# State-space stage: conditioning tiles at fixed places of TensorE's order, input groups by halves, an eighth of the tables on GpSimd

## The chip, the cores and the metric

The kernel runs on one core of a Trainium2 chip. TensorE multiplies matrices and transposes, VectorE (DVE) and ScalarE (ACT) work elementwise, GpSimd (POOL) does so too, SyncE (SP) issues most loads. The metric is the device time of one execution in microseconds. Before the change three runs took 1083.6, 1089.24 and 1095.2 us.

## What is computed

Two transformer blocks over 256 positions of 1024 channels. The first begins with a norm modulated by conditioning vectors (`ada`), a state-space mixer (S5) and its gated output, then a feed-forward stage (FFN), latent attention and a second FFN; the second block has a recurrent time mix and differential attention. The change lies in the mixer:

```python
u = modulate(rms_norm(x, norm1_g), shift, scale)      # conditioning
s[t] = a * s[t-1] + bb @ u[t]                         # 64 complex states per group of 16 channels
y = Re(c @ s) + d_skip * u
g = gelu(y); mix = g * sigmoid(g @ w_glu + b_glu)     # GLU
```

Of `ada` come shift and scale of the norm (8 tiles, `adaH`), the gates and the modulation of the FFN (16 tiles, `ada0`), and further on those of the other stages (`kvada`, `ada1`, ...).

## The kernel before, in words

**The stage.** `s5()` unrolls the recurrence into chunks of 8 positions. A loop over e = 0 to 7 (four of 32 input groups each) makes on VectorE the table P (FP, the factors, times s5bc, the input matrices: four products and two sums a step, lines L803ff), turns it on TensorE into Bm, multiplies it with the output matrices (`cbd`) into KTr, and takes conditioning tiles by `pump` (L829). GpSimd makes the output tables CE (L831ff). The modulated input `xs` is transposed to U (L843ff). `into(j2)` multiplies U with Bm, `turnG(j2)` transposes the result and ScalarE copies it to GT; `pipe` runs the two over j2 = 0 to 3, turnG a step behind. ScalarE then loads its table for the Gelu (L886). The scan (L888 to L920) is a chain of products and sums on VectorE over the states St. `kernels(i)`, i = 0 to 3, builds the matrices Kmat within a chunk from KTr: transposes, a split into `kparts` (cast on ScalarE, rest on VectorE), 14 shifting matmuls, copies by ScalarE. Then TensorE adds up U times Kmat and St times CE (`outputs`), ScalarE applies the Gelu (gT), which is split in two (`gh` on ScalarE, `gl` = gT - gh on VectorE, L422), and `proj` runs the GLU: 192 matmuls on `gh`, `gl` and the likewise split weights `whi` (ScalarE), `wlo` (VectorE).

**The conditioning tiles.** 24 tiles of 1 MB, `adaH` and `ada0`, are each used in four matmuls into `ps_gv` (`gemv_rows`, `gemv`). Each `pump()` takes the next; a ring of three buffers `raw` holds them, so tile n + 3 is loaded when tile n has been used. Behind them come tiles that are accumulated on VectorE instead (`acc`, L323), the first of them `kvada`; `self.after` names an instruction behind which those have to stay.

**What sets the order.** A scheduler orders each engine's instructions by its own estimates; TensorE's alone stands as written within `manual_schedule` (the tables' loop up to the end of `pipe`, and the outputs with the Gelu's transposes). `tc.issue_after(x)` lets what is inside be issued behind x. Engines take their instructions in order: one that waits holds up those behind it. SP's loads of the stage are one queue. A buffer's next load waits until its last user is done; the GLU's weights lie where the states (`A`) and the tables (`CE`) lay.

In the rows L327 is a matmul, L330 a transpose, L306, L323 and L319 are VectorE's elementwise operations, L298 and L376 ScalarE's activations and casts, L357 the load of a weight tile.

Of the kernel before, what the change touches and what calls it, by code (L numbers as in the profile page):

```python
# [9 lines left out]
F32 = mybir.dt.float32  # L10
# [6 lines left out]
D, T, FF = 1024, 256, 2816  # L17
# [43 lines left out]
O_ORDER = [0, 1, 2, 3, 6, 7, 4, 5]  # L61

# [73 lines left out]
def pack(inp):  # L136
# [4 lines left out]
    a["xs"] = x.reshape(32, 8, 4, 16, 16)[:, ::-1].transpose(2, 0, 3, 1, 4).reshape(128, WT)  # L141
# [3 lines left out]
    w = ada[0][:, :2048].reshape(8, 128, 2, 4, 256).transpose(0, 1, 3, 2, 4)  # L145
# [6 lines left out]
    hb = adb[0][:2048].reshape(2, 4, 256).transpose(1, 0, 2).reshape(4, 512)  # L152
    a["modH"] = np.concatenate([rep(hb), rep(i["norm1_g"][0].reshape(4, 256))], 1)
# [135 lines left out]
class K:  # L289
# [130 lines left out]
    def split(self, hi, lo, src, eng=None):  # L420

        self.nc.scalar.copy(out=hi, in_=src)  # L422
        self.sub(lo, src, hi.bitcast(F32), eng)
# [221 lines left out]
    def s5(self):  # L645
# [3 lines left out]
        with ExitStack() as ctx:  # L649
# [130 lines left out]
            def kernels(i):  # L780
# [8 lines left out]
                self.pump()  # L789
                for t2 in (5, 3, 1, 0):  # L790
                    if t2 in (1, 3):
                        self.pump()
# [10 lines left out]
            self.pump()  # L803
            for e in range(8):
                Pq = B8("P", [128, 2, 4, 8, 16], "P", 4)
                g4 = slice(4 * e, 4 * e + 4)
                fv = lambda r: FP[:, r, :, g4].rearrange("p t g -> p g t").unsqueeze(3).to_broadcast([128, 4, 8, 16])
                bv = lambda r: bc[:, r, g4, :].unsqueeze(2).to_broadcast([128, 4, 8, 16])
                for r, (b0, b1, op) in enumerate(((0, 1, ALU.subtract), (1, 0, ALU.add))):
                    m1 = self.ps().rearrange("p (g t e) -> p g t e", g=4, t=8)  # L810
# [18 lines left out]
                self.pump(2 if e % 3 == 1 else 1)  # L829

            CE = [[B8("CE", [128, 16, 8, 16], f"CE{r}{i}", 4) for i in range(2)] for r in range(2)]
            for e in range(8):
# [3 lines left out]
                for r, (p0, p1) in enumerate(((0, 1), (2, 0))):  # L836
# [4 lines left out]
                    self.sub(ce, ce, m1, G)  # L841

# [4 lines left out]
            for h in range(2):  # L847
# [4 lines left out]
                for j4 in range(2):  # L852
# [4 lines left out]
                    o = U[:, 8 * h + 4 * j4:8 * h + 4 * j4 + 4].rearrange("p j n -> p (j n)")  # L857
                    (S_.copy if j4 else V.tensor_copy)(out=o, in_=pt)
# [16 lines left out]
            def turnG(j2):  # L875
                pt = self.ps("aux")
                for jl in range(2):
                    for ri in range(2):
                        self.T(pt[:, 128 * (2 * ri + jl):128 * (2 * ri + jl) + 128], gs_[j2][:, jl, ri, :])
# [4 lines left out]
            self.pipe(4, [into, turnG])  # L884
            order.close()
            self.table(AF.Gelu_apprx_tanh)  # L886
# [8 lines left out]
            S_.copy(out=St[:, 1::8], in_=GT[:, 0::8])  # L895
# [26 lines left out]
            for i in range(4):  # L922
                kernels(i)
# [1331 lines left out]
```

## Time and profile before

| | before |
|---|---|
| three runs, median | 1089.24 us (1083.6 to 1095.2) |
| the profiled execution | 1079.3 us |
| its span, first to last instruction | 1077.5 us |
| mean granted TensorE clock | 0.98 |
| TensorE busy | 985.0 us (91%) |
| VectorE busy | 809.5 us (75%) |
| ScalarE, GpSimd busy | 580.3 and 268.9 us |

The profile describes one execution. Times in the rows are microseconds from the span's start. A timeline row gives start, length, engine, line, operation, output and inputs with the size of one operation; equal operations that follow one another are merged (x8); in brackets stands how long the engine was idle before it and what released it. The clock is a share of 2.4 GHz, its full level; 0.50 is 1.2 GHz.

### The profile page before, as it was taken

Reading aid. Unit: us, or ns where it says so; the run is one execution under the profiler, and the core shown is the slowest. Engines: PE = TensorE matmul, PEld = TensorE weight load, DVE = VectorE, ACT = ScalarE, POOL = GpSimd, SP = SyncE. Lnnn points to the kernel's source line nnn. Section 1 sums busy time; section 2 is a strip of 40 time slices with the busy share of each in tenths; the row PEclk is TensorE's granted clock in tenths of the full one; section 3 lists DMA queues with packets and bytes.
Section 4 is the critical chain, followed back from the end, with each engine's and each line's share of the span. In section 5 each row is a group of like instructions: output and inputs, shape, how many; then the busy total and the mean of one; then the engine's idle time right before and its main releaser. Section 6 shows DMA issues by size and latency. Waiting matters only on the chain.

```text
span 1077.5 us, 21985 instructions
## 1 busy us (share of the span) xinstructions
PE 985.0 (91%) x8490; PEld 876.3 (81%) x8490; DVE 809.5 (75%) x1771; ACT 580.3 (54%) x1301; POOL 268.9 (25%) x300
## 2 busy tenths in 40 slices
PE   3988979999999988989999999988898899799996
PEld 1446968989999866889999999987887786699984
DVE  8846788989985788779756555688887735686995
ACT  6344555556544767646555544565444344575663
POOL 7960200030011551100000001453315132243430
PEclk9999989999999989999999999999999999999999
DMA  7999439877983241255755554241312142265321
GB/s 280 375 343 372 172 142 396 307 285 294 363 329 153 98 162 73 79 196 203 267 192 174 184 195 152 104 148 54 123 40 83 36 154 99 87 232 180 134 79 40
DMA packets 29416, 198.82 MB, mean 185 GB/s; under 512 B 3744, under 2 KB 3872, under 8 KB 6528
## 3 DMA queue, kind: packets, MB, share of 16 engines
q1 hardware_dynamic: 27936, 191.73, 48.2%
q10 hardware_dynamic: 720, 3.15, 0.8%
q0 software_dynamic: 656, 2.53, 0.7%
q8 instruction: 67, 1.10, 0.4%
q14 instruction: 37, 0.30, 0.1%
HBM read 195.30 MB, written 2.10 MB: 183 GB/s over the span
## 4 chain that ended last, share of the span: by engine, by line
PE 65%; DVE 15%; issue 4%; ACT 3%; POOL 2%; DMA 1%; POOLq 0%; DVEq 0%; ACTq 0%
PE ps_mm L327 50%; PE ps_aux L327 6%; DVE wlo L306 3%; PE ps_sv L327 3%; PE ps_el L327 2%; PE ps_aux L330 2%; PE ps_st L327 2%; ACT whi L376 1%; POOL sq L306 1%; DVE Upr L306 1%; DVE acc L323 1%; DMA raw<-in_gu 1%; DVE D L1738 1%; DVE shf L319 1%; DVE A L306 0%
## 5 line engine op out<-in xcount | busy, mean ns | idle before, releaser
L376 ACT CAST whi<-raw 128x512 fp32r<-128x512 f32 (+2 forms) x488 | 296.1, 613 | 271.5 <-PE ps_mm L327 230.0
L306 DVE TENSOR_TENSOR wlo<-raw,whi 128x512 fp32r<-128x512 f32 (+2 forms) x412 | 289.1, 714 | 128.4 <-ACT whi L376 127.7
L327 PE MATMUL ps_mm<-hh,whi 128*128 128x256 f32 x1064 | 306.8, 290 | 3.0 <-ACT hh L298 2.3
L327 PE MATMUL ps_mm<-hh,wlo 128*128 128x256 f32 x1064 | 300.6, 285 | 3.4 <-DVE wlo L306 3.3
L327 PE MATMUL ps_mm<-hl,whi 128*128 128x256 f32 x1064 | 300.0, 283 | 0.2
L327 PEld LDWEIGHTS ps_mm<-hh,whi 128*128 128x128 f32 x1064 | 202.0, 190 | 8.2 <-ACT hh L298 2.9
L327 PEld LDWEIGHTS ps_mm<-hh,wlo 128*128 128x128 f32 x1064 | 200.9, 190 | 8.8 <-DVE wlo L306 7.8
L327 PEld LDWEIGHTS ps_mm<-hl,whi 128*128 128x128 f32 x1064 | 201.9, 190 | 1.3 <-DVE hl L323 0.6
L306 POOL TENSOR_TENSOR wlo<-raw,whi 128x512 fp32r<-128x512 f32 (+2 forms) x76 | 100.3, 1321 | 244.1 <-ACT whi L376 218.5
L306 POOL TENSOR_TENSOR sq<-sq 128x256 f32<-128x256 f32 x20 | 23.4, 1171 | 415.0 <-ACT sq L298 264.7
L327 PE MATMUL ps_mm<-ah,whi 128*128 128x256 f32 x352 | 99.1, 282 | 0.0
L327 PE MATMUL ps_mm<-ah,wlo 128*128 128x256 f32 x352 | 99.0, 282 | 0.1
L327 PE MATMUL ps_mm<-al,whi 128*128 128x256 f32 x352 | 98.8, 281 | 0.0
L323 DVE SCALAR_TENSOR_TENSOR acc<-raw,cs,acc 128x512 f32<-128x512 f32 x112 | 80.0, 757 | 2.2 <-DMA raw<-in_kvada 2.1
L327 PEld LDWEIGHTS ps_mm<-ah,wlo 128*128 128x128 f32 x352 | 66.3, 189 | 2.8 <-issue 1.7
L327 PEld LDWEIGHTS ps_mm<-ah,whi 128*128 128x128 f32 x352 | 67.3, 191 | 0.9 <-ACT whi L376 0.8
L327 PEld LDWEIGHTS ps_mm<-al,whi 128*128 128x128 f32 x352 | 66.4, 189 | 0.0
L327 PE MATMUL ps_gv<-raw,crep 128*32 128x512 f32 x192 | 27.3, 624 | 17.0 <-DMA raw<-in_adaH 13.7
L327 PEld LDWEIGHTS ps_gv<-raw,crep 128*32 128x32 f32 x192 | 4.5, 110 | 22.0 <-DVE pwt L306 13.7
L327 PE MATMUL ps_mm<-gl,whi 128*128 128x256 f32 x64 | 18.9, 297 | 2.4 <-DVE gl L306 2.4
L327 PE MATMUL ps_mm<-whi,ch 128*128 128x512 f32 x48 | 19.5, 437 | 1.2 <-ACT ch L422 1.2
L306 POOL TENSOR_TENSOR CE<-CE,cem 128x512 f32<-128x512 f32 x16 | 20.5, 1321 | 0.0
(552 smaller groups left out, 2037.3 us busy)
## 6 DMA issues: line engine op xcount, KB each, us to landing
raw<-in_gu SPq DMA_DIRECT2D x44, 1024.0 KB, 5.1
raw<-in_ada SPq DMA_DIRECT2D x32, 1024.0 KB, 7.2
raw<-in_dn SPq DMA_DIRECT2D x22, 1024.0 KB, 5.0
raw<-in_win SPq DMA_DIRECT2D x15, 1024.0 KB, 4.9
raw<-in_adaH SPq DMA_DIRECT2D x8, 1024.0 KB, 6.4
raw<-in_kvada SPq DMA_DIRECT2D x8, 1024.0 KB, 6.5
raw<-in_ada1h SPq DMA_DIRECT2D x8, 1024.0 KB, 5.7
raw<-in_wout SPq DMA_DIRECT2D x8, 1024.0 KB, 4.9
```

The source lines that it names most:

```text
L306: return (eng or self.nc.vector).tensor_tensor(out=out, in0=a, in1=b, op=op)
L319: (eng or self.nc.vector).tensor_scalar(out=out, in0=a, scalar1=s1, scalar2=s2, op0=op0, **kw)
L323: return self.nc.vector.scalar_tensor_tensor(out=out, in0=a, scalar=s, in1=b, op0=op0, op1=op1, **kw)
L327: return self.nc.tensor.matmul(out, l, r, start=start, stop=stop, **kw)
L330: return self.nc.tensor.transpose(out, in_, self.ident)
L376: i = self.nc.scalar.copy(out=hi[:, :width], in_=raw[:, o:o + width])
L1738: V.tensor_reduce(out=D_[64 * h:64 * h + 64, 4 * i:4 * i + 4], in_=dm[:, :, h].rearrange("p c b i -> p c i b"), axis=AX.X, op=ALU.add)
```

## The change

- **Conditioning tiles.** The tables' loop takes one tile per step (8, and one ahead of it) instead of one or two; `pipe` becomes a loop over its five steps with a tile behind each, in TensorE's fixed order; kernels(1) to (3) take three, three and two. The last two of the 24 are taken within the GLU.
- **kernels(0)** is split: its transposes (`latest(0)`) stand behind step 5 of the tables' loop, its 14 matmuls behind step 7, both in the fixed order. kernels(1) to (3) follow the scan in the program and lie behind the last transposes of turnG.
- **Tables.** Step 3 of the eight (`GP`) is made on GpSimd, from `FPs`, a copy of FP that ScalarE makes. GpSimd's CE follows it.
- **Halves.** `S5_ORDER` permutes input columns, on the host, so that the first half of `xs` holds what into(0) and into(1) need. U is copied by ScalarE alone.
- **Order.** The load of the Gelu's table follows the copy into St; the scan's instructions follow turnG's last transposes. `self.after` is set before the GLU to the last split: no accumulation on VectorE goes before it.

```diff
--- before.py
+++ after.py
@@ -59,6 +59,10 @@
 O_ORDER = [0, 1, 2, 3, 6, 7, 4, 5]
+
+S5_ORDER = [0, 1, 2, 3, 8, 9, 10, 11, 4, 5, 6, 7, 12, 13, 14, 15]
+
+GP = 3
@@ -138,19 +142,19 @@
-    a["xs"] = x.reshape(32, 8, 4, 16, 16)[:, ::-1].transpose(2, 0, 3, 1, 4).reshape(128, WT)
+    a["xs"] = x.reshape(32, 8, 4, 16, 16)[:, ::-1].transpose(2, 0, 3, 1, 4)[:, :, S5_ORDER].reshape(128, WT)
     a["xT"] = x.T.reshape(8, 128, T).transpose(1, 0, 2).reshape(128, WT)
...
     ada, adb = i["ada_w"], i["ada_b"]
-    w = ada[0][:, :2048].reshape(8, 128, 2, 4, 256).transpose(0, 1, 3, 2, 4)
+    w = ada[0][:, :2048].reshape(8, 128, 2, 4, 16, 16).transpose(0, 1, 3, 2, 4, 5)[:, :, :, :, S5_ORDER]
     a["adaH"] = w.reshape(8, 128, WT)
...
     rep = lambda m: np.repeat(m, 32, axis=0)
-    hb = adb[0][:2048].reshape(2, 4, 256).transpose(1, 0, 2).reshape(4, 512)
-    a["modH"] = np.concatenate([rep(hb), rep(i["norm1_g"][0].reshape(4, 256))], 1)
+    hb = adb[0][:2048].reshape(2, 4, 16, 16).transpose(1, 0, 2, 3)[:, :, S5_ORDER].reshape(4, 512)
+    a["modH"] = np.concatenate([rep(hb), rep(i["norm1_g"][0].reshape(4, 16, 16)[:, S5_ORDER].reshape(4, 256))], 1)
     col = lambda v: v.reshape(-1, 128).T
@@ -420,7 +424,7 @@
         self.nc.scalar.copy(out=hi, in_=src)
-        self.sub(lo, src, hi.bitcast(F32), eng)
+        return self.sub(lo, src, hi.bitcast(F32), eng)
@@ -777,7 +781,9 @@
-            def kernels(i):
+            kps = {}
+
+            def latest(i):
@@ -786,9 +792,13 @@
                 S_.copy(out=KM[i][:, 7].rearrange("p j n -> p (j n)"), in_=pt[:, :256])
-                self.pump()
+                kps[i] = kp
+
+            def kernels(i, pumps):
+
+                kp = kps[i]
                 for t2 in (5, 3, 1, 0):
-                    if t2 in (1, 3):
+                    if t2 in pumps:
                         self.pump()
@@ -801,12 +811,22 @@
             self.pump()
+            at = {}
+            FPs = x0[:, 5:7].rearrange("p r (t g) -> p r t g", t=8)
+            S_.copy(out=FPs, in_=FP)
             for e in range(8):
...
                 g4 = slice(4 * e, 4 * e + 4)
-                fv = lambda r: FP[:, r, :, g4].rearrange("p t g -> p g t").unsqueeze(3).to_broadcast([128, 4, 8, 16])
+                own = e == GP
+                fv = lambda r: (FPs if own else FP)[:, r, :, g4].rearrange("p t g -> p g t").unsqueeze(3).to_broadcast([128, 4, 8, 16])
                 bv = lambda r: bc[:, r, g4, :].unsqueeze(2).to_broadcast([128, 4, 8, 16])
                 for r, (b0, b1, op) in enumerate(((0, 1, ALU.subtract), (1, 0, ALU.add))):
+                    if own:
+                        m1 = sm.tile([128, 4, 8, 16], F32, tag="cem", name="Pm", bufs=2)
+                        self.mul(Pq[:, r], fv(0), bv(b0), G)
+                        self.mul(m1, fv(1), bv(b1), G)
+                        at["P"] = self.tt(Pq[:, r], Pq[:, r], m1, op, G)
+                        continue
                     m1 = self.ps().rearrange("p (g t e) -> p g t e", g=4, t=8)
@@ -826,9 +846,14 @@
                 S_.copy(out=KTr[:, e], in_=psK[:, :128])
-                self.pump(2 if e % 3 == 1 else 1)
+                self.pump()
+                if e == 5:
+                    latest(0)
+            kernels(0, [])
             CE = [[B8("CE", [128, 16, 8, 16], f"CE{r}{i}", 4) for i in range(2)] for r in range(2)]
+            behind = ctx.enter_context(ExitStack())
+            behind.enter_context(tc.issue_after(at["P"].ins))
             for e in range(8):
@@ -839,6 +864,7 @@
                     self.sub(ce, ce, m1, G)
+            behind.close()
@@ -854,8 +880,8 @@
                         self.T(pt[:, 128 * j:128 * j + 128], xs[:, jj].rearrange("p s e -> p (s e)"))
-                    o = U[:, 8 * h + 4 * j4:8 * h + 4 * j4 + 4].rearrange("p j n -> p (j n)")
-                    (S_.copy if j4 else V.tensor_copy)(out=o, in_=pt)
+                    o = U[:, 8 * j4 + 4 * h:8 * j4 + 4 * h + 4].rearrange("p j n -> p (j n)")
+                    S_.copy(out=o, in_=pt)
@@ -876,14 +902,16 @@
                     for ri in range(2):
-                        self.T(pt[:, 128 * (2 * ri + jl):128 * (2 * ri + jl) + 128], gs_[j2][:, jl, ri, :])
+                        at["T"] = self.T(pt[:, 128 * (2 * ri + jl):128 * (2 * ri + jl) + 128], gs_[j2][:, jl, ri, :])
                 for ri in range(2):
...
-            self.pipe(4, [into, turnG])
+            for _ in self.steps(4, [into, turnG]):
+                self.pump()
             order.close()
-            self.table(AF.Gelu_apprx_tanh)
+            later = ctx.enter_context(ExitStack())
+            later.enter_context(tc.issue_after(at["T"].ins))
@@ -892,7 +920,9 @@
             S_.copy(out=A8[:, 1], in_=QP[:, 1:3, 0])
-            S_.copy(out=St[:, 1::8], in_=GT[:, 0::8])
+            i = S_.copy(out=St[:, 1::8], in_=GT[:, 0::8])
+            with tc.issue_after(i.ins):
+                self.table(AF.Gelu_apprx_tanh)
             for k in range(1, 8):
@@ -919,8 +949,10 @@
                 self.add(o, o, w1[:, 1])
-            for i in range(4):
-                kernels(i)
+            for i in range(1, 4):
+                latest(i)
+                kernels(i, (5, 3, 1)[i == 3:])
+            later.close()
@@ -968,7 +1000,7 @@
                 for k in range(4 * q2, 4 * q2 + 4):
-                    self.split(gh[:, k], gl[:, k], gT[:, k].rearrange("p t c -> p (t c)"))
+                    self.lowed = self.split(gh[:, k], gl[:, k], gT[:, k].rearrange("p t c -> p (t c)"))
@@ -978,7 +1010,7 @@
             x1 = x0
-
+            self.after = self.lowed
             add, root = self.sumsq()
```

TensorE from the last step of the tables' loop to the last transposes of turnG; `ps_gv` is a conditioning tile, Gs what `into` gave. Before:

```order
L327 MATMUL ps_gv<-raw,crep 32x512 x8
L330 MATMUL ps_aux<-c_cst_75,xs 128x128 x12
L327 MATMUL ps_gv<-raw,crep 32x512 x4
L330 MATMUL ps_aux<-c_cst_75,xs 128x128 x4
L327 MATMUL ps_aux<-Bm_238,U 32x2x64 x16
L327 MATMUL ps_gv<-raw,crep 32x512 x4
L330 MATMUL ps_aux<-c_cst_75,Gs 128x128 x4
```

And with the change:

```order
L331 MATMUL ps_gv<-raw,crep 32x512 x4
L331 MATMUL ps_aux<-kparts,shift 128x256 x14
L334 MATMUL ps_aux<-c_cst_75,xs 128x128 x16
L331 MATMUL ps_mm<-Kmat_242,U 32x128
L331 MATMUL ps_aux<-Bm_238,U 32x2x64 x16
L331 MATMUL ps_gv<-raw,crep 32x512 x4
L331 MATMUL ps_mm<-Kmat_242,U 32x128 x7
L334 MATMUL ps_aux<-c_cst_75,Gs 128x128 x4
```

Two tiles have left the place ahead of into(0), and kernels(0)'s 14 matmuls (`kparts,shift`) have come there.

VectorE from the copy of the outputs (`ys`) on, at the start of the GLU. Before:

```order
L960 COPY ys<-ps_mm 128x4x8x16
L319 TENSOR_SCALAR acc<-raw,cs 128x512 x4
L306 TENSOR_TENSOR wlo<-raw,whi 128x512 x2
L323 SCALAR_TENSOR_TENSOR acc<-raw,cs,acc 128x512 x3
L306 TENSOR_TENSOR gl<-gT,gh 128x256
L323 SCALAR_TENSOR_TENSOR acc<-raw,cs,acc 128x512
L306 TENSOR_TENSOR gl<-gT,gh 128x256 x3
```

And with the change:

```order
L992 COPY ys<-ps_mm 128x4x8x16
L310 TENSOR_TENSOR wlo<-raw,whi 128x512 x2
L310 TENSOR_TENSOR gl<-gT,gh 128x256 x4
L310 TENSOR_TENSOR wlo<-raw,whi 128x512
L992 COPY ys<-ps_mm 128x4x8x16
```

The eight accumulations have left this place, and with them the load that the four `gl` stood behind.

SP's loads behind those of the tables. Before:

```order
L357 DMA raw<-in_ada 128x2048 x16
L357 DMA raw<-in_wglu 128x2048
L938 DMA x<-in_xT 128x2048
L357 DMA raw<-in_wglu 128x2048
L357 DMA raw<-in_kvada 128x2048
L357 DMA raw<-in_wglu 128x2048
L357 DMA raw<-in_kvada 128x2048
```

And with the change:

```order
L361 DMA raw<-in_ada 128x2048 x14
L970 DMA x<-in_xT 128x2048
L361 DMA raw<-in_wglu 128x2048 x2
L361 DMA raw<-in_ada 128x2048
L361 DMA raw<-in_wglu 128x2048
L361 DMA raw<-in_ada 128x2048
L361 DMA raw<-in_wglu 128x2048
```

Two tiles of `ada0` have come between the GLU's loads; those of kvada have gone behind them.

## Rows read from the trace of the kernel before

**Rows 1.** Windows: stretch, length, busy PE, PEld, DVE, ACT, POOL, clock, DMA share, GB/s.
```profile
16.00:50.00 34.00, 29.03 (x292) 16.11 (x292) 33.21 (x53) 17.98 (x43) 33.53 (x45) 1.00 0.81 318
50.00:68.00 18.00, 14.80 (x210) 7.83 (x210) 4.22 (x7) 6.61 (x14) 18.00 (x16) 1.00 0.95 356
68.00:94.00 26.00, 22.31 (x227) 12.92 (x231) 20.93 (x55) 13.73 (x30) 3.72 (x4) 1.00 0.93 346
```

**Rows 2.** Waits of PE, 16 to 70 us: total, times, longest.
```profile
PE ps_gv L327 <- DMA raw<-in_ada: 3.2, 4, 1.4
```

**Rows 3.** Timeline of PE, the transposes of the last two steps of turnG.
```profile
63.52 0.66 PE L330 MATMUL ps_aux<-c_cst,Gs 128*128 128x128 f32 x4
...
66.11 0.66 PE L330 MATMUL ps_aux<-c_cst,Gs 128*128 128x128 f32 x4
```

**Rows 4.** Timeline of ACT, the load of the Gelu's table.
```profile
67.84 1.28 ACT L298 ACT_TABLE_LOAD   x1
```

**Rows 5.** Timeline of DVE, from the scan.
```profile
70.42 0.42 DVE L306 TENSOR_TENSOR u<-St,ps_aux 128x256 f32<-128x256 f32 x1
...
75.05 0.42 DVE L306 TENSOR_TENSOR kparts<-ps_aux,kparts 128x256 fp32r<-128x256 f32 x1 [0.52 <-ACT kparts L786]
...
92.98 0.17 DVE L306 TENSOR_TENSOR mods<-ps_aux,c_cols 128x16 f32<-128x16 f32 x1 [1.14 <-PE ps_aux L639]
93.07 0.61 DVE L306 TENSOR_TENSOR St<-St,w 128x448 f32<-128x448 f32 x1
```

**Rows 6.** Timeline of PE, outputs and start of the GLU.
```profile
95.08 1.08 PE L327 MATMUL ps_mm<-Kmat,U 128*32 128x128 f32 x32
...
104.27 0.39 PE L327 MATMUL ps_mm<-gh,whi 128*128 128x256 f32 x1
107.04 0.39 PE L327 MATMUL ps_mm<-gl,whi 128*128 128x256 f32 x1 [2.39 <-DVE gl L306]
...
109.31 0.39 PE L327 MATMUL ps_mm<-gh,wlo 128*128 128x256 f32 x1 [1.52 <-DVE wlo L306]
```

**Rows 7.** Timeline of DVE, accumulations ahead of `gl`.
```profile
104.58 2.08 DVE L323 SCALAR_TENSOR_TENSOR acc<-raw,cs,acc 128x512 f32<-128x512 f32 x3 [2.11 <-DMA raw<-in_kvada]
```

**Rows 8.** Windows of 1 us in the GLU, columns as in the first group.
```profile
110.00:111.00 1.00, 1.00 (x7) 1.00 (x7) 0.46 (x1) 0.00 (x0) 0.00 (x0) 0.50 0.00 0
...
113.00:114.00 1.00, 1.00 (x12) 1.00 (x11) 0.65 (x2) 1.00 (x3) 0.00 (x0) 0.99 1.05 442
```

**Rows 9.** Tile P on DVE, 14 to 50 us: ns min/median/max, first and last start.
```profile
L306 DVE TENSOR_TENSOR P<-ps_mm,s5bc x16: 675/675/691, 15.2 to 41.6; 128x512 f32<-128x512 f32 x16
L306 DVE TENSOR_TENSOR P<-P,ps_mm x16: 629/674/677, 19.4 to 43.4; 128x512 f32<-128x512 f32 x16
```

**Rows 10.** Timeline of DVE, the modulation of `xs`.
```profile
44.45 4.86 DVE L306 TENSOR_TENSOR xs<-xs,ps_mm 128x1024 f32<-128x1024 f32 x4
```

**Rows 11.** Timeline of ACT, the sixth of eight squarings of the input.
```profile
15.95 0.42 ACT L298 ACTIVATE junk<-xs 128x256 f32<-128x256 f32 x1
```

**Rows 12.** Timeline of PE, P's transposes in steps 4, 5 and 6.
```profile
36.11 1.09 PE L330 MATMUL ps_aux<-c_cst,P 128*128 128x128 f32 x8
...
39.91 1.09 PE L330 MATMUL ps_aux<-c_cst,P 128*128 128x128 f32 x8
...
42.85 1.09 PE L330 MATMUL ps_aux<-c_cst,P 128*128 128x128 f32 x8
```

**Rows 13.** Timeline of POOL, the last tables, and sums of squares much later.
```profile
69.15 2.57 POOL L306 TENSOR_TENSOR CE<-CE,cem 128x512 f32<-128x512 f32 x2
...
222.45 7.63 POOL L306 TENSOR_TENSOR sq<-sq 128x256 f32<-128x256 f32 x5 [81.84 <-PE ps_mm L327]
```

**Rows 14.** Timeline of DVE, accumulations beside those sums of squares.
```profile
228.30 3.67 DVE L323 SCALAR_TENSOR_TENSOR acc<-raw,cs,acc 128x512 f32<-128x512 f32 x4
```

**Rows 15.** Loads issued at 94.6 and at 110.5 us: KB, us to landing.
```profile
raw<-in_wglu SPq DMA_DIRECT2D x1, 1024.0 KB, 12.0
...
raw<-in_kvada SPq DMA_DIRECT2D x1, 1024.0 KB, 4.8
```

**Rows 16.** A window in the feed-forward stage's down half, columns as in the first group.
```profile
330.00:340.00 10.00, 10.00 (x87) 9.80 (x86) 5.87 (x11) 4.67 (x10) 2.08 (x2) 1.00 0.33 126
```

## The prediction

> **What bounds the kernel now.** The change touches the state-space stage and its gated output projection (GLU), roughly the first 135 us. I read in this order: busy time by stretch, TensorE's waits, the timelines of TensorE, VectorE and ScalarE, then the queues of GpSimd and the loads.
>
> From 16 to 50 us VectorE is full, 33.21 of 34 us: it makes the P tables [rows 1]. From 50 to 68 it works 4.22 of 18 us and TensorE 14.80: transposes, the products of `into` and a conditioning tile per step, with waits for the tiles' loads of 3.2 us in all [rows 1, 2]. From 68 to 94 neither engine is full (20.93 and 22.31 of 26); the end is set by the scan, one chain on VectorE, into which pieces of other work are put [rows 1, 5]. Its last add ends at 93.07 + 0.61 = 93.7. From there TensorE needs 10.6 us to the GLU's first matmul at 104.27, which holds 1.08 us of matmuls on Kmat that don't need the scan [rows 6]. Then it stands 2.39 us for `gl` and 1.52 us for `wlo` [rows 6]: ahead of `gl`, VectorE's queue has accumulations of the kvada tiles, which wait 2.11 us for a load [rows 7]. While TensorE stood still its clock fell: 0.50 of full at 110 us, 7 matmuls per us where there are 12 at 113 us [rows 8].
>
> **The change, part by part.** Times are those of the profiled execution, 1079.3 us with 1077.5 in the span.
>
> *Tables.* The rows that write P start between 15.2 and 43.4 us; with 16 products written to PSUM they are 48 operations in 44.1 - 15.2 = 28.9 us, 0.60 each [rows 9]. Six go to GpSimd, so 42 remain: 25.2 us. But GpSimd reads a copy that ScalarE makes of FP, and in the changed order VectorE's first product waits for it. The copy stands behind five of the eight squarings, where the sixth now starts at 15.95 [rows 11]; 512 elements by the 0.42 us of 256 are an estimated 0.6 to 0.8. P starts at about 16.6, 1.4 later. After 38 operations and a reciprocal VectorE is at 39.6, and there the subtraction `kparts` of kernels(0) now stands ahead of the last five. It needs two transposes on TensorE behind step 5 of the table loop. That step began at 39.91; a step with two tiles takes 39.91 - 36.11 = 3.80, one with a single tile 42.85 - 39.91 = 2.94 [rows 12]. Two double steps before it become single (-1.7) and the start slips 1.4, so it begins at about 39.4, the transposes come at 42.3, and the subtraction ends near 43.2. Five operations (3.0), the modulation (0.4) and `xs` (4.86) end at 51.6, where `xs` ended at 44.45 + 4.86 = 49.3 [rows 10]. **The table stage gets 2.3 us longer**, although six operations left it. If nothing stopped VectorE it would be shorter by 1.0, and TensorE would then bind at about 50.5: that is the lower bound.
>
> *Kernels(0) and the steps of `into`.* Its 14 matmuls stand ahead of the transposes of `xs`, in the time in which TensorE waits for `xs`: free, unless `xs` comes before 51. All 16 transposes stand ahead of into(0), so the order by halves by itself brings no earlier start. The last eight (1.09 like eight of the tables [rows 12]) and a copy put into(0) at 53.3. One tile per step, with three buffers filled beforehand, needs one load of about 2.4 us (below) per step of 66.11 - 63.52 = 2.59 [rows 3]: the waits of 3.2 us go. 53.3 and 2.3 to the first transposes, three steps of 2.59: the last at 63.4 and not 66.11, **2.7 earlier**.
>
> *Table load of ScalarE.* It ran at 67.84, 1.7 after the last transposes, for 1.28 us [rows 4]. Now the scan's first column is copied first; but kparts(1) stands behind the scan's first product on VectorE and waits for a cast that is behind the load. 65.1 for the last copies, 0.4, 1.5, 0.35 and 0.4 give the second product at 67.7, before 70.42 [rows 5]: **2.7 earlier**, so the moved load gives nothing. Without that wait it would be 1.4 more.
>
> *Scan.* It took 93.7 - 70.42 = 23.3. kparts(1) inside it goes (0.52 wait and 0.42), and the second `mods` (1.14 wait, 0.1) moves into the GLU, since the last two tiles are taken there [rows 5]: 21.1 remain and the scan ends at 88.8, **4.9 earlier**. That needs TensorE to be through three kernels and eight tiles by then: one tile more (1.0) and one kernel less (about 2) than its 22.31 us in 26 [rows 1]; it fits 25 us with little to spare.
>
> *From the scan to the GLU.* Kmat's 1.08 us now lie ahead of the scan's end: first GLU matmul at 98.3, **6.0 earlier**.
>
> *In the GLU.* Accumulations may no longer precede the splits, so the two waits of 3.9 us go, and with them the half clock: some 20 matmuls at 1/7 and not 1/12 us, 1.2 to 1.8. New are eight matmuls for two tiles (2.0), transposes (0.5) and waits. The GLU's loads go out only at the scan's end, since their buffer is that of its states. A load alone lands after 4.8 us; one with three ahead after 12.0, so 2.4 each in a row [rows 15]. The order is GLU, GLU, tile, GLU, tile: 93.6, 96.0, 98.4, 100.8, 103.2. TensorE wants the last tile at about 103 and then `gl` of the second half, split behind other work of ScalarE: 1.0 to 2.0 of waits. In all -5.4 + 4.0: **about 1.7 gained, bounds 0 and 3**.
>
> *Behind the GLU* nothing of its tail changes. Two tiles of accumulation (2.1 us for three operations [rows 7]) go to the feed-forward stage; its gate half keeps its 18 tiles, the two go to the down half, where VectorE works 5.87 of 10 us [rows 16]: nothing, with 5.5 us as the price if that slack were not there.
>
> **Sum.** 6.0 and 1.7 are 7.7, with rounding 8: 1079.3 becomes 1071.3. The three timed runs lie at 1083.6 to 1095.2 around 1089.24, above the profiled one; by the same 8 us their median becomes **1081 us**.
>
> *A rule weighed.* GpSimd's tables end at 69.15 + 2.57 = 71.7 [rows 13]. Six operations of at most 1.3 go in front of them, so they end near 79.5; they are wanted from 88.8. Beside the sums of squares that GpSimd ran from 222.45 to 230.1, four accumulations took 3.67 us (0.92 each) where three took 2.08 (0.69) [rows 7, 13, 14]: 0.9 us lost in 1.8 of overlap, half. The page "GPSIMD Engine Reference" of the Trainium skill, section Key points, says that GpSimd shares its SBUF interfaces with VectorE and that they collide with VectorE instructions that read two SBUF inputs; these rows agree. VectorE's P operations read PSUM and one SBUF input, so the six cost it nothing. The last third of the scan adds and multiplies out of SBUF alone, from about 80.5 on: it starts one microsecond after GpSimd ends.
>
> **Rivals.** (1) *More*: VectorE isn't stopped by kparts(0) and kparts(1) as I read it, or the GLU waits for less. For it: these waits are worked out of an order, with margins of half a microsecond; against it: each is a queue in which nothing may overtake. 1.0 or 1.4 and 1.5: about 12 us gained, 1077. (2) *GpSimd late*, the tables colliding with the scan's last third, or TensorE late with the kernels: 5 us of overlap cost 2.5 us, up to 4 with the outputs late; 1084. It decides from 1 us of delay. (3) *Slower*: the first GLU tile lands late. Three casts of it stand in ScalarE's queue ahead of the Gelu of the first half, so GLU matmuls come 3.8 us after its landing or at 98.3, whichever is later. Landing after 12.0 and not 4.8 us: 104.6, so 6.3 lost, the clock falls in that pause (1.2 to 1.8), and the second tile is late too (0.9): some 9 lost, 1090, just slower. It decides from 11 us. For it: before, the first GLU tile had landed before the scan ended; against it: nothing is left in the queue then. (4) *Nothing*: the table stage, which the change is about, doesn't shorten at all by the working above; the gain comes from the tiles' places. If TensorE still waits for tiles, 3.2 go, 1084 as in (2).
>
> **How the numbers follow.** Forecast 0.50 (own range 1078 to 1085), (1) 0.28, (2) and (4) 0.14, (3) 0.08. Run to run this kernel moves by 6 us either way, a median by perhaps 4. Low: 12 us gained and 7 of spread and unknowns, 1070; high: case (3) and 2, 1092. About 1% (11 us) is what a measurement of this kernel can tell from no change. Faster than 1078.3: a quarter of the forecast and two thirds of (1), 0.31. Slower than 1100: 0.06. The rest, 0.63.
>
> **What would show it.** P begins near 16.6, `xs` ends near 51.6, TensorE's waits for in_ada in the steps are gone, the scan ends near 89, the first GLU matmul comes near 98 without the pause and without the half clock, GpSimd ends its tables before 81. It is wrong if the scan ends after 91, if the first GLU tile lands after 95, or if the feed-forward stage gives back more than 2 us.

## The result and the profile after

| | before | after | ratio [95%] |
|---|---|---|---|
| first comparison, medians of 4 runs each | 1087.76 us (1083.6 to 1095.2) | 1073.47 us (1071.1 to 1074.85) | 0.9881 [0.9839, 0.9922] |
| second comparison, 26 and 6 runs | 1084.07 us (1079.19 to 1089.38) | 1074.59 us (1069.84 to 1076.48) | 0.9909 [0.988, 0.9938] |
| profiled execution | 1079.3 us | 1071.1 us | |

The changed kernel is faster by 0.9 to 1.2%: 1073.5 us where 1081 was forecast, inside the range 1070 to 1092. The two profiled executions lie 8.2 us apart, forecast 8.0; the medians lie 9.5 and 14.3 us apart. The clock's mean is 0.986 (0.98 before).

Where the 8.2 us lie, with the forecast's own times:

| us from the span's start | before | forecast | after |
|---|---|---|---|
| VectorE's first P product | 15.2 | 16.6 | 15.8 |
| `xs` ends | 49.3 | 51.6 | 51.2 |
| last transposes of turnG | 66.1 | 63.4 | 62.4 |
| second product of the scan | 70.4 | 67.7 | 66.8 |
| scan ends | 93.7 | 88.8 | 89.3 |
| first GLU matmul | 104.3 | 98.3 | 98.6 |
| first matmul of the feed-forward stage | 142.9 | | 135.0 |

Timeline of TensorE, answering to [rows 3, 6] (line numbers have moved by four: L331 is a matmul, L334 a transpose):

```profile
50.70 2.02 PE L334 MATMUL ps_aux<-c_cst,xs 128*128 128x128 f32 x16
...
59.94 0.66 PE L334 MATMUL ps_aux<-c_cst,Gs 128*128 128x128 f32 x4
...
62.42 0.66 PE L334 MATMUL ps_aux<-c_cst,Gs 128*128 128x128 f32 x4
...
66.33 1.89 PE L331 MATMUL ps_gv<-raw,crep 128*32 128x512 f32 x8 [1.88 <-DMA raw<-in_ada]
...
97.55 1.10 PE L331 MATMUL ps_mm<-CE,St 64*32 64x128 f32 x28 [0.29 <-issue]
98.59 0.39 PE L331 MATMUL ps_mm<-gh,whi 128*128 128x256 f32 x1
...
100.32 1.06 PE L331 MATMUL ps_gv<-raw,crep 128*32 128x512 f32 x8 [0.88 <-DMA raw<-in_ada]
...
103.09 1.03 PE L334 MATMUL ps_aux<-c_cst,ys 128*128 128x128 f32 x8
...
105.30 1.07 PE L331 MATMUL ps_gv<-raw,crep 128*32 128x512 f32 x8 [0.58 <-DMA raw<-in_ada]
```

The steps of `into` follow one another every 2.48 us without a wait. One wait for a tile is left, 1.88 us, but behind turnG; the GLU has two short ones. The waits for `gl` and `wlo` are gone.

Timeline of VectorE, answering to [rows 5, 7, 10]:

```profile
15.77 0.69 DVE L310 TENSOR_TENSOR P<-ps_mm,s5bc 128x512 f32<-128x512 f32 x1 [1.23 <-ACT x L816]
...
42.51 0.42 DVE L310 TENSOR_TENSOR kparts<-ps_aux,kparts 128x256 fp32r<-128x256 f32 x1 [4.47 <-ACT kparts L792]
...
46.30 4.86 DVE L310 TENSOR_TENSOR xs<-xs,ps_mm 128x1024 f32<-128x1024 f32 x4
...
66.46 0.43 DVE L310 TENSOR_TENSOR kparts<-ps_aux,kparts 128x256 fp32r<-128x256 f32 x1 [1.35 <-ACT kparts L792]
66.80 0.41 DVE L310 TENSOR_TENSOR u<-St,ps_aux 128x256 f32<-128x256 f32 x1
...
79.87 1.73 DVE L310 TENSOR_TENSOR v<-St,QP 128x64 f32<-128x64 f32 x2
...
88.02 1.27 DVE L310 TENSOR_TENSOR St<-St,w 128x448 f32<-128x448 f32 x2
...
97.93 1.43 DVE L310 TENSOR_TENSOR gl<-gT,gh 128x256 fp32r<-128x256 f32 x4 [1.60 <-ACT gh L426]
```

VectorE loses what GpSimd took from it: it waits 1.23 us for ScalarE's copy and 4.47 us for `kparts` of kernels(0).

Windows of after: stretch, length, busy PE, PEld, DVE, ACT, POOL, clock, DMA share, GB/s, as [rows 1]:

```profile
16.00:50.00 34.00, 29.03 (x288) 17.04 (x289) 29.43 (x49) 18.87 (x46) 33.53 (x40) 1.00 0.74 273
50.00:66.00 16.00, 14.44 (x225) 9.16 (x223) 4.43 (x7) 10.05 (x21) 16.00 (x15) 1.00 0.79 303
66.00:90.00 24.00, 21.81 (x246) 11.94 (x250) 21.29 (x51) 8.78 (x20) 15.38 (x14) 0.93 0.84 323
66.00:68.00 2.00, 1.67 (x8) 0.16 (x8) 1.47 (x4) 0.80 (x3) 2.00 (x3) 0.61 0.85 320
68.00:70.00 2.00, 2.00 (x12) 1.13 (x12) 1.84 (x5) 0.59 (x1) 2.00 (x3) 0.54 1.01 414
...
98.00:112.00 14.00, 12.54 (x116) 10.28 (x108) 6.49 (x14) 6.29 (x15) 0.00 (x0) 1.00 0.77 318
```

Up to 50 us VectorE is no longer full (29.43 of 34, before 33.21); TensorE's share is what it was. At half clock (1.2 GHz) TensorE is now only from 66 to 70 us, behind the 1.88 us pause; in the GLU it has the full clock, where [rows 8] showed half.

### The profile page after: what moved, and what is told of

The parts are those of the page before. It is cut to its first block, busy times and chain, and to the rows that moved or that the text cites. A ratio compares the mean times of both kernels' runs of the same rounds, so it can differ in the third digit from the quotient of the medians.

```text
span 1069.3 us, 21987 instructions
## 1 busy us (share of the span) xinstructions
PE 980.3 (92%) x8490; PEld 873.8 (82%) x8490; DVE 803.8 (75%) x1763; ACT 581.6 (54%) x1304; POOL 274.2 (26%) x306
## 4 chain that ended last, share of the span: by engine, by line
PE 69%; DVE 18%; issue 4%; ACT 3%; POOL 2%; DMA 2%; POOLq 0%; DVEq 0%; ACTq 0%
PE ps_mm L331 50%; PE ps_aux L331 7%; DVE wlo L310 3%; PE ps_aux L334 3%; PE ps_sv L331 3%; PE ps_el L331 2%; DMA raw<-in_ada 2%; PE ps_st L331 2%; PE ps_gv L331 1%; ACT whi L380 1%; DVE Upr L310 1%; POOL sq L310 1%; DVE D L1770 1%; DVE St L310 1%; DVE acc L327 0%
## 5 line engine op out<-in xcount | busy, mean ns | idle before, releaser
L331 PE MATMUL ps_mm<-hh,whi 128*128 128x256 f32 x1064 | 307.2, 290 | 3.2 <-ACT hh L302 2.5
L331 PE MATMUL ps_mm<-hh,wlo 128*128 128x256 f32 x1064 | 300.8, 285 | 3.6 <-DVE wlo L310 3.6
L331 PE MATMUL ps_mm<-hl,whi 128*128 128x256 f32 x1064 | 300.9, 283 | 0.5
L331 PEld LDWEIGHTS ps_mm<-hh,wlo 128*128 128x128 f32 x1064 | 200.9, 190 | 9.7 <-DVE wlo L310 7.7
L331 PEld LDWEIGHTS ps_mm<-hh,whi 128*128 128x128 f32 x1064 | 202.1, 190 | 7.8 <-ACT hh L302 2.9
L331 PEld LDWEIGHTS ps_mm<-hl,whi 128*128 128x128 f32 x1064 | 202.2, 190 | 1.9 <-DVE hl L327 1.2
L331 PE MATMUL ps_mm<-ah,whi 128*128 128x256 f32 x352 | 99.1, 282 | 0.0
L331 PE MATMUL ps_mm<-al,whi 128*128 128x256 f32 x352 | 98.8, 281 | 0.0
L331 PE MATMUL ps_mm<-ah,wlo 128*128 128x256 f32 x352 | 98.7, 282 | 0.0
L331 PEld LDWEIGHTS ps_mm<-ah,whi 128*128 128x128 f32 x352 | 67.3, 191 | 0.9 <-ACT whi L380 0.8
L331 PEld LDWEIGHTS ps_mm<-ah,wlo 128*128 128x128 f32 x352 | 66.3, 189 | 1.7 <-issue 0.8
L331 PEld LDWEIGHTS ps_mm<-al,whi 128*128 128x128 f32 x352 | 66.5, 189 | 0.0
L331 PE MATMUL ps_gv<-raw,crep 128*32 128x512 f32 x192 | 28.2, 654 | 17.2 <-DVE ps_mm L310 13.7
L331 PEld LDWEIGHTS ps_gv<-raw,crep 128*32 128x32 f32 x192 | 4.5, 112 | 20.0 <-DVE ps_mm L310 13.7
L331 PE MATMUL ps_mm<-whi,ch 128*128 128x512 f32 x48 | 19.5, 437 | 1.2 <-ACT ch L426 1.2
L310 DVE TENSOR_TENSOR Upr<-NB,Us 128x16 f32<-128x16 f32 (+14 forms) x45 | 16.9, 376 | 4.5 <-ACT NB L1787 3.0
```

The lines of the kernel that those rows point to most:

```text
L310: return (eng or self.nc.vector).tensor_tensor(out=out, in0=a, in1=b, op=op)
L331: return self.nc.tensor.matmul(out, l, r, start=start, stop=stop, **kw)
```

## The experiments

Two theories were open: **A**, the prediction's steps are the gain, and the larger difference of the medians is chance; **B**, the kernel before loses more in most of its executions than in the one that was profiled. Beside them: which of the parts carry the gain.

**1, 2. Both kernels again, unaltered** (`again`, `before_again`).

> The changed kernel once more, unaltered. The two profiled executions differ by 8.2 us (1079.3 and 1071.1), the medians of the timed runs by 13 to 14. Theory A (the change is worth what the profiles show, the rest is scatter of the kernel before): ratio 0.9925 (8.2 of 1088), and runs of the kernel before as low as 1080. Theory B (the timed runs of the kernel before hold a loss that its profiled execution was spared): ratio 0.988, 13 us, with no run of before under 1083.

> The kernel before, unaltered, for what a comparison scatters and for a second profile of it. Both theories: ratio 1.000 within 0.003. Theory A: its stage has the same times as in the first profile (first GLU matmul 104.3, first feed-forward matmul 142.9, each within 0.5) and differences of whole runs come from elsewhere. Theory B: where the run is 5 us or more longer than 1079.3, the stage itself is longer, with the loss around the GLU (a longer pause or more time at the half clock).

1074.59 us, ratio 0.9909 [0.988, 0.9938], and 1085.13 us, 1.0013 [0.9992, 1.0034]. The difference of the medians is 9.5 us, between the two theories, and the interval holds both. Neither holds as it was put: 9 of the 26 runs of before lie below 1083 us, against B, and between the two traces of before the first GLU matmul differs by 4.3 us and the first feed-forward matmul by 5.2, against A. The traces show where: in this execution of the kernel before (span 1088.7) TensorE's transposes of `xs` start 2.4 us later than in the first. Its timeline:

```profile
50.32 1.07 PE L327 MATMUL ps_gv<-raw,crep 128*32 128x512 f32 x8
52.78 1.07 PE L327 MATMUL ps_gv<-raw,crep 128*32 128x512 f32 x8 [1.39 <-DMA raw<-in_ada]
53.77 1.53 PE L330 MATMUL ps_aux<-c_cst,xs 128*128 128x128 f32 x12
55.84 0.64 PE L327 MATMUL ps_gv<-raw,crep 128*32 128x512 f32 x4 [0.54 <-DMA raw<-in_ada]
```

`xs` ended at 49.24; two tiles stand between it and its transposes, and for one of them TensorE waits. In the first execution it waited as long (1.4 us, [rows 2]), but for a tile that came 2.4 us earlier. Three traces of the old front (the third is of run 3) begin these transposes at 51.4, 53.8 and 54.9 and end the scan at 93.7, 97.7 and 97.0; the two of the changed kernel begin at 50.7 and 50.6 and end at 89.3 and 90.0. Two traces show little of a spread: with four later kernels that have the same front (runs 6, 7, their combination, and 8) the six begin at 50.1 to 51.8 and end the scan at 89.2 to 90.0.

Not all of the loss lies ahead of the transposes. In run 3 the 3.3 us are there at turnG's end (69.4 for 66.1); in `before_again` 1.6 are (67.7), and the other 2.4 are lost within the scan, where VectorE waits for `kparts` (0.52 us in [rows 5]) while TensorE's clock is at 0.50 from 72 to 76 us:

```profile
79.07 0.42 DVE L306 TENSOR_TENSOR kparts<-ps_aux,kparts 128x256 fp32r<-128x256 f32 x1 [2.91 <-ACT kparts L786]
```

The place that B named is wrong: the GLU takes 39.5 us there and 38.6 in the first execution. The profiled execution of before lies at the low end of what the 26 runs show (1079.3, lowest 1079.19).

**3. Only the order in the GLU** (`glu_alone`). The kernel before, with the one line on `self.after`:

```diff
-        self.sub(lo, src, hi.bitcast(F32), eng)
+        return self.sub(lo, src, hi.bitcast(F32), eng)
-                    self.split(gh[:, k], gl[:, k], ...)
+                    self.lowed = self.split(gh[:, k], gl[:, k], ...)
+            self.after = self.lowed
```

> The kernel before with one part of the change: accumulations on VectorE may not go before the last split of the GLU (self.after), nothing else. Theory (the 2.39 and 1.52 us of waits and the half clock behind them come from the accumulations ahead of gl): the scan and the first GLU matmul stay (93.7 and 104.3), the two waits go, the first feed-forward matmul comes 4 to 5.5 us earlier (137.4 to 138.9 for 142.9), ratio about 0.9955. Rival (the accumulations are only put off and hold up wlo or the tail within the GLU): the same waits later in the GLU, first feed-forward matmul within 1 us of 142.9, ratio 1.000.

1077.74 us, 0.9943 [0.9924, 0.9962]: 6 us. Both waits are gone, and from the first GLU matmul to the feed-forward stage it takes 34.2 us where the kernel before takes 38.6. By its place in time alone the end would speak for the rival, since the first feed-forward matmul comes at 141.95, within 1 us of 142.9; but the front was 3.3 us late in this execution (scan end 97.0, not the 93.7 that was expected), and the stretch from the GLU on decides. In the medians of this comparison more than half of the whole gain, 6.3 of 9.5 us, is this line. The changed kernel takes 36.4 there, since two tiles are now among these matmuls.

**4. Without the share of GpSimd** (`no_gpsimd_share`). The changed kernel with

```diff
-GP = 3
+GP = 8
-            S_.copy(out=FPs, in_=FP)
-            behind.enter_context(tc.issue_after(at["P"].ins))
```

> The changed kernel without GpSimd's eighth of the tables: all 48 operations on VectorE, no copy of FP, GpSimd's output tables from the start as before. Theory (VectorE stands for the subtraction of kernels(0) until about 42.5 in any case, 4.47 us of it idle): xs ends within 0.5 us of 51.2, the scan's end within 0.7 of 89.2, and the time is that of the changed kernel within 1 us. Rival (VectorE's tables still set the start): six operations come back, 3.6 us, less the 1.2 us of waiting for the copy: xs ends 2.4 us later and so does everything behind it; 2.4 us slower than the changed kernel.

The front was near what the theory said: `xs` ends at 51.64, the scan at 90.05, 0.5 and 0.8 us behind the changed kernel. But the time was 1078.85 us, 0.9948 [0.9929, 0.9967], 4.3 us slower than the changed kernel, which neither side had. TensorE's timeline shows it in the GLU:

```profile
101.43 1.07 PE L331 MATMUL ps_gv<-raw,crep 128*32 128x512 f32 x8 [1.11 <-DMA raw<-in_ada]
...
106.46 1.94 PE L331 MATMUL ps_gv<-raw,crep 128*32 128x512 f32 x8 [3.96 <-DMA raw<-in_ada]
...
110.41 1.44 PE L334 MATMUL ps_aux<-c_cst,ys 128*128 128x128 f32 x8
```

The scheduler, whose own estimates had shifted a little, put both tiles ahead of the transposes of the Gelu's second half: these come at 110.4, not 103.1, and behind the 3.96 us pause the clock is at half (0.50 from 106 to 110 us). That the place and not the share cost the time was a guess here; runs 8 to 11 test it.

**5. `kparts` of kernels(0) three steps earlier** (`kparts_early`): `if e == 2:` for `if e == 5:` in the changed kernel.

> The changed kernel with the transposes of kernels(0) behind step 2 of the tables' loop and not step 5, so that VectorE no longer stands 4.47 us for its subtraction. Theory (the front is bound twice: behind VectorE stands TensorE's chain with the eighth adaH tile, whose copy comes at 45.8): the wait is gone, xs still ends between 50.5 and 51.2, scan and GLU come at most 0.5 us earlier, ratio to the kernel before as that of the changed kernel, 0.991 within 0.002. Rival (the stop of VectorE is what the front costs): xs ends near 47, everything behind it 3 to 4 us earlier, ratio 0.987.

1072.81 us, 0.99 [0.9879, 0.992]: no measurable gain. The wait of 4.47 us is gone, and a row of VectorE's timeline shows another in its place:

```profile
45.42 0.43 DVE L327 SCALAR_TENSOR_TENSOR ps_mm<-ps_mm,modH 128x256 f32<-128x256 f32 x1 [3.93 <-ACT ps_mm L678]
```

The modulation of `xs` needs the eight adaH tiles, and with one per step the last is used in the loop's last step. `xs` ends at 50.74. The front is bound twice. What it gained further on is lost again in the scan: its products `v` start at 78.42, 1.45 us earlier than in the changed kernel, but stand until GpSimd's tables end at 81.50, and the scan ends at 89.41 for 89.29 (rows in the last section).

**6. Tiles of the GLU ahead of it** (`tiles_before_scan_end`): `(5, 3, 1)` for `(5, 3, 1)[i == 3:]` and one more `pump()` behind the kernels, so that no tile is left for the GLU.

> The changed kernel with the last two conditioning tiles not in the GLU but among kernels(3), as far as TensorE's order goes. Theory (in the GLU the two cost 2.0 us of matmuls, 0.5 of transposes and 1.5 of waits for loads, nothing hides them; ahead of the scan's end TensorE has 0.4 us to spare, so 1.6 to 2 us of them come back there): first GLU matmul at 100.2 to 100.8 and not 98.6, GLU 4 us shorter, first feed-forward matmul 2 us earlier than the 135.0 of the changed kernel, ratio 0.989. Rival (the tiles hold up the outputs in full, or the Gelu's transposes, and the GLU's loads behind them): first feed-forward matmul at 135 or later, ratio 0.991 or above.

1076.32 us, 0.9929 [0.9904, 0.9953]: no gain. The scheduler put the two tiles among the outputs (at 93.70 and 96.37); the GLU starts at 101.77, 3.2 later, and is 2.9 shorter, so that the feed-forward stage starts at 135.26, as the rival has it. The edit didn't bring them ahead of the scan's end, so that place remains untried.

**7. The Gelu's table loaded later** (`table_load_late`): the load behind kparts(1)'s cast, not ahead of it.

> The changed kernel with ScalarE's table load behind the cast of kparts(1) and not ahead of it. Theory (the scan's second product waits for that cast, and TensorE's chain ends 0.4 us ahead of the scan): second product at 65.3 and not 66.8, scan's end up to 1.4 earlier on VectorE, but the outputs start only 0.4 to 1.0 earlier, since TensorE then sets their start; ratio 0.990. Rival (the load comes in the way of the copies behind it and TensorE waits): outputs at the same time or later, ratio 0.991 or above.

1073.73 us, 0.9909 [0.9885, 0.9932]: no measurable gain. From turnG's last transposes to the scan's second product it takes 2.95 us in place of 4.38, the 1.4 that the prediction had for it. But `xs` ended 1.1 us later in this execution (52.27), so the product comes at 66.49 and not at 65.3; and TensorE had half clock from 68 to 76 us, so that its own chain is through only at 90.53, where the outputs start, 1 us behind the scan's end at 89.49. With edit 6 added (`tiles_and_table`) the time was 1076.94 us, 0.9935 [0.9917, 0.9954], where 0.988 was expected if the two gains add up and 0.989 if not: both missed.

**8 to 10. The GLU in one fixed order.** In three kernels the two tiles of the GLU may only be issued behind the second half's transposes:

```diff
-                    for g in range(n): self.mm(ps[32 * g:...], ...)
+                    with self.tc.issue_after(self.hold.ins) if self.hold is not None else ExitStack():
+                        for g in range(n): self.mm(ps[32 * g:...], ...)
-                        self.T(pt[:, 128 * tl:...], ys[...])
+                        self.hold = self.T(pt[:, 128 * tl:...], ys[...])
```

`hold` is the changed kernel with this, `no_share_hold` run 4's kernel, and `places_hold` the kernel before with the tiles' places and the line of run 3 alone: no share on GpSimd, kernels(0) whole and behind turnG, no halves.

> The changed kernel with one thing more: the matmuls of the two conditioning tiles inside the GLU may only be issued behind the transposes of the Gelu's second half. In the kernel without the GpSimd share, 4.3 us slower, these transposes stood behind both tiles. Theory A, that the tiles' loads set the time: the last of the two lands at about 105 whatever stands ahead of it; TensorE now waits 1.5 to 3 us for it at about 102.5 and gets the two waits of 0.9 and 0.6 back: the same time as the changed kernel within 1.5 us, ratio to the kernel before 0.988 to 0.992. Theory B, that the tiles hold up the second half of the Gelu: 1.5 to 3 us faster than the changed kernel, 0.986 to 0.988.

> The changed kernel without the GpSimd share, and with the same hold, so that its GLU stands in the same order as in the run with the hold alone. Theory: the share of the tables on GpSimd is worth 0.5 us at most, and what made the kernel without it 4.3 us slower was only the place of the two tiles: within 1 us of the run with the hold alone, scan end near 90. Rival: GpSimd's share itself is worth about 4 us in a way that the front's times do not show: 0.994 to 0.996 of the kernel before, as without the hold.

> The kernel before with only: one tile per step of the tables' loop and of the into loop in the fixed order, two tiles per kernels(i), these behind the last transposes of turnG, the two last tiles within the GLU and held as in the other two runs, no accumulation before the splits. No GpSimd share, no split of kernels(0), no order by halves, the table load where it was. Theory: the places of the tiles and the order in the GLU carry the whole gain: xs ends at 49.3 and its transposes start at 49.5 to 50, with no wait for tiles ahead of them, the last turnG transposes come at 62 to 62.5, the scan ends at 89 to 90, and the time is within 1.5 us of the run with the hold alone (about 0.989 of the kernel before). Rival: kernels(0) back within the scan, the GpSimd share and the halves are worth 2 us or more: scan end at 91 or later, 0.992 to 0.995.

`hold` 1072.79 us, 0.9903 [0.9888, 0.9918]: the time of the changed kernel, theory A. `no_share_hold` 1070.55 us, 0.9879 [0.9862, 0.9895]: the 4.3 us are back, with 2 more. So run 4 lost them by the place, and the share on GpSimd brings no gain that these runs show; the scan ends at 90.22. Rows of its GLU, to be held against run 4's:

```profile
103.43 1.03 PE L334 MATMUL ps_aux<-c_cst,ys 128*128 128x128 f32 x8
104.39 1.06 PE L331 MATMUL ps_gv<-raw,crep 128*32 128x512 f32 x8
106.52 1.06 PE L331 MATMUL ps_gv<-raw,crep 128*32 128x512 f32 x8 [1.06 <-DMA raw<-in_ada]
```

`places_hold` 1075.63 us, 0.9916 [0.9897, 0.9936]: 2.8 us behind `hold` in the median and 1.2 in the profiled execution, with intervals that overlap: more than the theory's 1.5 us, less than the rival's 0.992. The expected 49.3 for the end of `xs` was a miss: it is 51.26, though no `kparts` stops VectorE and nothing of its work lies on GpSimd. As in run 5 the modulation waits for its data, which the loop with one tile per step gives later (row of VectorE's timeline):

```profile
45.93 0.43 DVE L323 SCALAR_TENSOR_TENSOR ps_mm<-ps_mm,modH 128x256 f32<-128x256 f32 x1 [1.85 <-ACT ps_mm L675]
```

TensorE, earlier than `xs` here, waits 2.1 us for it and goes on at half clock (0.64 from 50 to 54 us), so turnG ends at 63.23 and the scan at 90.55. The tiles' places and the GLU's line carry most of the gain, some 8 of 11 us; whether the rest is worth anything the intervals leave open.

**11. The fastest again, with edit 5** (`no_share_hold_early`).

> The kernel of the run no_share_hold (1070.55 us, ratio 0.9879 [0.9862, 0.9895]) with one thing more: the transposes of kernels(0) stand behind step 2 of the tables' loop and not behind step 5, as in the run kparts_early. There the front was bound twice, so that this alone gave nothing in the time of the changed kernel. Without the GpSimd share VectorE has 48 operations for P and stops for `kparts` in between. Theory A, that this stop costs VectorE here: xs ends at 50.7 to 51.0 in place of 51.7, 0 to 1 us faster, ratio 0.9865 to 0.9885. Theory B, that the low time of no_share_hold was chance: back at 0.990 to 0.9915, the ratio of the changed kernel and of the run with the hold alone.

1073.27 us, 0.9899 [0.9873, 0.9925]: next to theory B, though the interval holds both. What `no_share_hold` was faster than the changed kernel is not confirmed. A's step failed: `xs` ended at 51.84, not at 51, since VectorE waits 2.11 us for the modulation's data as in run 5. Six runs with the whole order (1, 5, 7, 8, 9, 11) lie between 0.9879 and 0.9909; none beats the changed kernel by more than the runs can tell.

## Why the prediction was right, and where it wasn't

**Right by its steps.** On the profiled pair each time in the table came within 1.0 us, the sum within 0.2. `xs` does end later (51.2) although six operations left VectorE. The wait for `kparts`, the reason given, stands there (4.47 us), but it is one of two: without it the modulation's data come at 45.4 to 45.9 and `xs` ends at 50.7 (run 5) and 51.3 (`places_hold`). The working had a lower bound near that, 50.5, and said only that TensorE would bind there. The steps of `into` lose their waits. The GLU gains 2.25 us on the pair (38.63 to 36.38) where 1.7 was put, bounds 0 and 3; run 3 shows 4.4 for the waits and the half clock, against 5.4, and against run 3 the changed kernel's GLU is 2.2 us longer, where 4.0 were put for the two tiles. Nothing is given back in the feed-forward stage. Of the rivals, *slower* asked for a first GLU tile that lands after 11 us; it landed 4.8 us after its issue at 89.4.

**Where it was luck.** That the sum came within 0.2 us is in part chance. The GLU's own terms, -5.4 and +4.0, make 1.4 and not 1.7, so the sum is 7.4 before rounding. turnG ended 1.0 us early and the scan took 1.4 longer, which cancel. And 7.9 us are gained at the start of the feed-forward stage, 10.0 at its last matmul, 8.2 at the end of the kernel; rows of TensorE, before and after:

```profile
349.58 0.28 PE L327 MATMUL ps_mm<-ah,wlo 128*128 128x256 f32 x1
...
339.56 0.28 PE L331 MATMUL ps_mm<-ah,wlo 128*128 128x256 f32 x1
```

The stage took 206.7 us before and 204.6 after, but 206.5 in `again`: nothing in the working speaks of these 2 us, nor of the 1.8 that are lost behind the stage. Two slips of the table stage weigh nothing: 39.91 less 1.7 plus 1.4 is 39.6 and not 39.4, and 37 operations, not 38, stand ahead of `kparts`, where VectorE had to wait in any case.

**The step that failed: "by the same 8 us their median becomes 1081".** A difference worked out on one execution was put on a median 10 us above it. Most of what it missed is that base: 1089.24 was the median of three runs, and in the four later comparisons the kernel before has medians of 1083.6 to 1084.4. From 1084.07 the same 8 us give 1076, 1.5 us above the 1074.59 that was measured beside it. The step also assumed that what kept the other runs of before slower lay elsewhere. Part of it lay in the front: the traces of before spread by 3.4 us at the start of `xs`' transposes and by 4.0 at the scan's end, the six with the new front by 1.7 and 0.8. So the front is worth 4.4 us on the first pair and some 7 to 8 against the other two traces. How much of this the medians hold is open, since 9.5 us and the profiles' 8.2 differ by less than the interval. The rest of the difference between runs (in `before_again` 5.2 us are lost by the feed-forward stage's start and 6 behind it) isn't explained by these traces. Whether 0.31 for *faster* was low isn't settled either: the first comparison passes its line of 1% (0.9881), the second just misses it (0.9909).

**Terms that were mis-sized.** P starts at 15.8, not 16.6: ScalarE's copy took 0.57 us and started at 15.17, since the squarings ahead of it began 0.65 us earlier (12.61 for 13.26; the reason is in the last section). GpSimd ends at 81.4 and not 79.5: before, it made four tables in a gap at 11.64 us, which now stand behind its share; that gap was not in the working, and the sign that GpSimd ends before 81 was not met. The end then falls into the scan's last third, as rival 2 said, from which it "decides from 1 us of delay": it came 1.9 late, and `v`, a pair in the scan, took 1.73 us where it takes 0.36 undisturbed. It cost 1.4 us and not 2.5, since only 1.5 us of the tables fell into that part. [rows 13] ended at 71.7. "The waits of 3.2 us go": they go in the steps, but a step is 2.48 us and no longer 2.59, and the tile behind the last step follows after 1.6 us (63.01). The loads don't keep up: from 60 to 66 us the DMA engines are full with 385 to 442 GB/s, an estimated 2.4 to 2.7 us for 1 MB, and the load issued at 60 us lands after 6.2 us where the two before it took 4.8. So TensorE waits 1.88 us one tile later, at 66.33, with half clock behind it. In this execution the scan sets the end and it costs little; in `again` the wait is 2.51 us, the clock 0.50 from 68 to 76 us, and the scan ends 0.7 us later.

**Not in the working at all:** that the place of two tiles in the GLU against the Gelu's second half is worth 4 us and more (run 4 against `no_share_hold`), and that this place is the scheduler's choice, which an edit far ahead of it can move.

## To carry to other kernels

Where one engine's order holds loads of a ring, fix one per step: here it cost no busy time, and this stage's start spread by 1.7 us over six traces, not 3.4 over three. The spread of whole runs did not clearly shrink (6.6 us over the 6 runs of `again`, 10.2 over 26 of before). Before a profile's sum is put on a median, look where the profiled execution lies among the runs, how many runs the median has, and ask what of their spread the change itself removes. An experiment that takes one part away can let a scheduler move another: compare the order and the timeline of the rest before the difference is put down to the part.

## What the runs showed that was not expected

**A VectorE instruction that stood until GpSimd was through.** In the prediction the collision with GpSimd had been given a price of half the overlap. VectorE's `v`, 64 elements a row from two SBUF inputs, takes 0.21 us alone. Tile `v` on VectorE in the run `kparts_early` (ns min/median/max, first and last start):

```profile
L310 DVE TENSOR_TENSOR v<-St,QP x4: 209/210/3166, 78.4 to 84.5; 128x64 f32<-128x64 f32 x4
```

and the last tables of GpSimd there:

```profile
79.00 2.50 POOL L310 TENSOR_TENSOR CE<-CE,cem 128x512 f32<-128x512 f32 x2
```

`v` starts at 78.42 and both end at 81.72; GpSimd ends at 81.50. In the changed kernel the pair of `v` starts at 79.87 and ends at 81.60 (GpSimd 81.38), in `hold` 80.46 and 81.49 (81.27); in `again` it starts at 81.84, behind GpSimd, and takes 0.36. Until then VectorE's operations of the scan, each with an operand in PSUM, ran at 0.35 to 0.43 us beside the same tables. These rows agree with the rule weighed in the prediction (Trainium skill, "GPSIMD Engine Reference", Key points): what stood had two SBUF inputs.

In this place the price was the whole overlap. In five traces with the share the pair starts anywhere from 78.4 to 80.5 us and ends at 81.5 to 81.7, so GpSimd sets the scan's end there, and what the front gains on top is lost; in the other two (`again`, run 7) the scan arrives behind GpSimd. In the seven traces without the share GpSimd is through at 71.6 to 71.8, and the pair takes 0.36 us each time.

The trace of before had the collision too, ahead of P, where the prediction didn't look. VectorE's rows, before and after:

```profile
11.98 0.90 DVE L306 TENSOR_TENSOR PW<-pwt 128x128 f32<-128x128 f32 x1
...
11.95 0.28 DVE L310 TENSOR_TENSOR PW<-pwt 128x128 f32<-128x128 f32 x1
```

Before, GpSimd began its first table of the gap at 11.64, for 1.09 us; the instruction ends at 12.88, just behind it, and what follows on VectorE and ScalarE up to P is 0.6 us later than in the changed kernel, where those tables are gone from the gap. Here VectorE came through behind the first of four tables, in the scan only behind the last; why, no run shows.

**A pause that no data explains.** In the outputs TensorE stands still at one place of its instructions, "issue" in the rows: 0.29 us in the changed kernel, 0.38 before, 0.87 in `again`, 1.00 and 1.21 in `no_share_hold` and `places_hold`, 2.07 in `hold`, where the clock then fell to 0.52. The timeline of TensorE in `hold`:

```profile
96.25 1.32 PE L331 MATMUL ps_mm<-CE,St 64*32 64x128 f32 x36
99.64 1.10 PE L331 MATMUL ps_mm<-CE,St 64*32 64x128 f32 x28 [2.07 <-issue]
```

A packet of the instruction queue (16 KB) appears in the DMA records at 97.2 us in `hold`, 96.9 in `no_share_hold`, 95.7 in `kparts_early`, 95.2 in the changed kernel; TensorE goes on at 99.64, 99.29, 98.11 and 97.55, 2.4 us behind it each time, while the loads of the GLU keep the DMA full (1.02 from 97 to 99 us in `hold`). That TensorE waited for its own instructions behind these loads fits all four; no run took the loads away, so it is not shown.
